# A TensorE-bound kernel in three-term fp32r: tiles padded to lines of 256 bytes, and the last gate and up columns as one block

## The chip, the cores and the metric

The kernel runs on one core of one Trainium2 chip. The metric is the time of one execution on the device, in microseconds; where several runs are compared, their median.

The five engines run side by side and meet at semaphores. In the profile, PE is TensorE's matmuls and PEld its loads of the stationary operand; DVE is VectorE, ACT ScalarE, POOL GpSimd, and SP the engine that here only issues DMAs. PSUM, into which matmuls write, has eight banks for each partition; one bank holds 512 fp32 columns. SBUF is addressed by a partition and by a byte within it. "Residue" below is a start address within the partition modulo 256.

## What is computed

One batch of 256 tokens of width 1024 runs through three layers; each is a feed-forward part, a mixer and another feed-forward part, all in fp32. The feed-forward part has six uses, and its hidden width is 2816, that is five blocks of 512 columns and one of 256:

```python
D_FF = 2816
def swiglu(x, w_gate, w_up, w_down):
    return (jax.nn.silu(x @ w_gate) * (x @ w_up)) @ w_down
...
    for l in range(DEPTH):
        f1 = swiglu(rms_norm(x, ffn1_pre_g[l]), ffn1_w_gate[l], ffn1_w_up[l], ffn1_w_down[l])
        x = x + FFN_RESIDUAL_WEIGHT * rms_norm(f1, ffn1_post_g[l])
        m = token_mixer(rms_norm(x, mix_pre_g[l]), w_in[l], fox_forget_b[l],
...
        x = x + rms_norm(m, mix_post_g[l])
        f2 = swiglu(rms_norm(x, ffn2_pre_g[l]), ffn2_w_gate[l], ffn2_w_up[l], ffn2_w_down[l])
```

The mixer of the first layer holds two kinds of softmax attention; that of the two others has three branches (stick breaking, block attention, sparse attention), gates of 3 x 1024 columns and an output projection. For the change the mixers matter as more matrix products of the same form.

## The kernel before

**Tiling.** The tokens are two blocks `t` of 128. A weight matrix comes in units of 128 partitions (rows) times at most some 1024 columns of fp32, that is 512 KB: `wtiles` (L203) takes `step = 1100 // n` row tiles of `n` columns into one unit, so two row tiles for n = 512, four for n = 256 and four for n = 264. The down and output projections load one row tile of 1024 columns as a unit.

**Three terms.** A product in fp32 accuracy is made of three matmuls in fp32r. `load` (L186) brings a unit by one DMA from SP's queue (L190) into a buffer `raw`, ACT rounds it to `hi` (L198), and DVE subtracts to get `lo` (L200). The activations are split the same way into `xh` and `xl` (or `ah` and `al` in the down projection). `mm3` (L211) issues hi with xh (L213), lo with xh (L214) and hi with xl (L215). The weight tile is the moving operand, which streams through the array, 512 columns wide as a rule; the activation tile of 128 columns is the stationary one, loaded ahead of each matmul (PEld). A unit of 1024 columns is thus 12 matmuls of 512 columns: two halves, two token blocks, three terms. TensorE runs in the order written here, apart from small pieces of other work that the scheduler of the language puts between.

**Buffers and addresses.** `raw`, `hi` and `lo` have four buffers each (RAW, HILO), used in turn. A buffer is as large as the largest tile of its tag: the 4 x 264 columns of the forget gates' projection, 4224 bytes, which is 16.5 x 256. Small tiles that lie ahead (`mhalf` and `eps` of 4 bytes, `gT` of 32) shift all that follows. In the built program `xh` and `xl` begin at residue 32 (96 in one place of the mixers); `hi` and `lo` begin, buffer by buffer in turn, at 32, 160, 32, 160; `ah` and `al` begin at 224. The last four units of a down projection have buffers of their own (MORE), at 224. The columns of a tile are whole multiples of 256 bytes away from its start in nearly all these matmuls, so an operand has its tile's residue.

Units of 12 matmuls in a row with one weight tile, counted in the built program: in the gate and up columns of the feed-forward parts 108 at residue 32 and 108 at 160; in the down projections 42 at 32 and 42 at 160; in the gates and projections of the mixers 37 at 32 and 37 at 160. The rest are halves of six matmuls, where one token block goes ahead of the other: about 80 of them lie at 160.

**The feed-forward part** (`ffn`, L338). For each block of 512 columns gate (`g`) and up (`u`) are two `dense` products of 48 matmuls, into two PSUM tiles `mm` (three banks in turn) and two `at` (two banks). Then ACT makes `sg = silu(g)` (L362), DVE `a = u * sg` (L364). `flush` (L346) transposes the `a` of the block before on TensorE, four pieces for each token block into `tp` (two banks) and `po` (one bank), from which ACT casts `ah` (L252) and DVE makes `al` (L253); it runs between gate and up of the next block. The last block has 256 columns: 48 matmuls of 256 columns for gate, the transposes of block five, 48 of 256 for up, and then the transposes of the last block itself. `out_proj` (L671) follows with 22 units of 12 matmuls into two `mm` and two `at`.

Of the kernel before, what the change touches and what calls it, by code (L numbers as in the profile page):

```python
# [8 lines left out]
F32 = mybir.dt.float32  # L9
F32R = mybir.dt.float32r  # L10
BF = mybir.dt.bfloat16
# [5 lines left out]
P = 128  # L17
# [11 lines left out]
MORE = 4  # L29

# ---------------------------------------------------------------- constants that depend on shapes only
# [85 lines left out]
class K:  # L117
    def __init__(self, ctx, tc, d):
# [15 lines left out]
        self.x = []  # L134
        for t in range(2):
            xt = self.cpool.tile([P, D], F32, name=f"x{t}")
            nc.sync.dma_start(out=xt, in_=d["x"][0, t * P:(t + 1) * P, :])
            self.x.append(xt)
# [4 lines left out]
        self.mhalf = self.cpool.tile([P, 1], F32, name="mhalf")  # L143
        nc.vector.memset(self.mhalf, -0.5)
        self.eps = self.cpool.tile([P, 1], F32, name="eps")
        nc.vector.memset(self.eps, EPS)

    def consts(self):
        cf = self.cpool.tile([P, F32_W], F32, name="cf")
# [14 lines left out]
    def tile(self, pool, shape, tag, dt=F32, bufs=None):  # L164
        kw = {} if bufs is None else {"bufs": bufs}
        return pool.tile(shape, dt, tag=tag, name=self.nm(tag), **kw)
# [13 lines left out]
    def sm(self, w, tag="sm"):  # L180
        if tag == "rs":
            return self.tile(self.small, [P, w], tag)
        return self.tile(self.small, [P, 32 if w > 8 else 8], "sm32" if w > 8 else "sm", bufs=2 if w > 8 else 24)[:, :w]

    # ------------------------------------------------------------ weights
    def load(self, w, r0, nk, c0, n, pool=None):  # L186
        """rows r0.. (nk tiles of 128), cols c0..c0+n, split exactly into hi + lo."""
        nc = self.nc
        raw = self.tile(self.wpool, [P, nk, n], "raw", bufs=RAW)
        nc.sync.dma_start(out=raw, in_=w[r0:r0 + nk * P, c0:c0 + n].rearrange("(k p) n -> p k n", p=P))  # L190
# [12 lines left out]
    def wtiles(self, w, r0, nk, c0, n):  # L203
        """the K tiles of load(), one by one, in units of at most 1024 columns."""
        step = max(1, 1100 // n)
# [11 lines left out]
    def dense(self, ps, xs, w, c0, n, skew=False):  # L217
        """ps[t] = x[t] @ w[:, c0:c0 + n]; with skew token block 0 goes ahead of token block 1."""
# [14 lines left out]
    # ------------------------------------------------------------ norms  # L233
    def rsqrt(self, out, ss, scale, eps):
        """out = (ss * scale + eps) ** -0.5"""
# [9 lines left out]
    def split_T(self, src, hi, lo, k0=0, bank=None):  # L245
        """transpose 512 columns of src (f32, token-major) into hi/lo[:, k0:k0+4]."""
# [8 lines left out]
    def prenorm(self, t, g):  # L255
        """transposed x*g (hi, lo) and the per-token 1/rms."""
# [15 lines left out]
    def first_norms(self, gd):  # L272
        """prenorm() of both token blocks, the gain put on after the transposes."""
# [5 lines left out]
        gT = self.cpool.tile([P, 8], F32, name="gT")  # L279
# [26 lines left out]
    def prenorms(self, gd):  # L306
        """transposed inputs of a part; the part before has left them, but for the very first."""
# [5 lines left out]
    def finish(self, t, ps, weight, post):  # L313
        """x[t] += weight * (rmsnorm(f) * post, or f)."""
# [22 lines left out]
    # ------------------------------------------------------------ feed forward  # L337
    def ffn(self, gd, wg, gc0, wu, uc0, wd, postd, nxt):  # L338
# [3 lines left out]
        with tc.tile_pool(name=self.nm("ffn"), bufs=1) as fp:  # L342
# [8 lines left out]
            for c0 in range(0, FF, 512):  # L351
                n = min(512, FF - c0)
                ps = {}
                for name, w, base in (("g", wg, gc0), ("u", wu, uc0)):
                    for t in range(2):
                        ps[name, t] = self.mm((P, n)) if name == "g" else self.at((P, n))
                    self.dense([ps[name, t] for t in range(2)], xs, w, base + c0, n, c0 == 0 and name == "g")
                    if name == "g":
                        flush()
# [18 lines left out]
    # ------------------------------------------------------------ pieces of the mixers  # L378
    def small_gain(self, pool, g, reps, tag):
        """[P, reps, n] copy of a vector of n on every partition."""  # L380
# [16 lines left out]
    def rope(self, x, cos, sin, half):  # L397
        """x: [P, G, >=2*half] in place; cos, sin: [P, 2*half], sin with its sign."""
# [10 lines left out]
    def head_rs(self, sq, n):  # L409
        """1 / rms of the last axis, from the squares [P, G, n]: exp and ln, then a step of Newton's."""  # L410
# [14 lines left out]
    def head_norm(self, out, x, s, g):  # L425
        """out = rms norm of s * x over the last axis of [P, G, n], gains g; s: one scalar per token."""
# [766 lines left out]
```

## Time and profile before

| | |
|---|---|
| median of three runs | 1811.75 us (1810.66 to 1812.93) |
| the profiled execution: its time is its span, first to last instruction | 1813.0 us |
| PE busy | 1790.0 us, 99% |
| PEld busy | 1471.7 us, 81% |
| DVE busy | 1079.1 us, 60% |
| ACT busy | 895.2 us, 49% |
| DMA | 305 MB, mean 168 GB/s |

The profiled execution lies at the upper end of the three timed ones, 1.25 us above their median. Of a matmul the start is measured, and its end is modelled; matmuls overlap in the pipeline, so a duration of 0.39 us is not the time that one costs. What a matmul costs is the distance from its start to the start of the next, which the timeline gives to 0.01 us.

### The profile page before, as it was taken

The numbers are of one execution on the slowest core, as the hardware profiler recorded it, in microseconds if no ns is written. First come the engines' busy times: TensorE is split into PE (matmuls) and PEld (weight loads), VectorE is DVE, ScalarE is ACT, GpSimd is POOL, SyncE is SP. The second block draws the span as 40 slices with busy tenths as digits, with TensorE's granted clock in tenths as the row PEclk, the third lists the DMA queues.
The fourth block names the chain that finished last, engine by engine and source line by source line (L and its number), as shares of the span: only waits on it lengthen the run. The fifth ranks groups of instructions, "written<-read, shape, count | busy, mean of one in ns | idle before, by whom it ended". The sixth has DMA issues, their size and how long they took to land.

```text
span 1813.0 us, 23411 instructions
## 1 busy us (share of the span) xinstructions
PE 1790.0 (99%) x8875; PEld 1471.7 (81%) x8883; DVE 1079.1 (60%) x1705; ACT 895.2 (49%) x1358; POOL 25.9 (1%) x42
## 2 busy tenths in 40 slices
PE   8999999999999999999999999999999999999999
PEld 6888787788878888787888888888887878888887
DVE  5555565555555555797567555555556975575553
ACT  5444455444445444475555444444444755554442
POOL 0000100000000000000000000000000000000000
PEclk9999999999999999999999999999999999999999
DMA  8665644266556655544255665666555442546653
GB/s 271 185 185 184 189 134 147 83 205 180 183 186 187 185 177 183 155 141 127 71 174 176 207 186 177 201 180 182 178 185 156 140 129 70 174 163 207 181 181 128
DMA packets 154594, 305.11 MB, mean 168 GB/s; under 512 B 13641, under 2 KB 44945, under 8 KB 154481
## 3 DMA queue, kind: packets, MB, share of 16 engines
q1 hardware_dynamic: 154464, 303.61, 54.6%
q8 instruction: 70, 1.15, 0.3%
q14 instruction: 44, 0.35, 0.1%
q10 hardware_dynamic: 16, 0.00, 0.0%
HBM read 302.53 MB, written 1.05 MB: 167 GB/s over the span
## 4 chain that ended last, share of the span: by engine, by line
PE 93%; DVE 3%; DMA 2%; ACT 1%; issue 1%; SPq 0%; POOL 0%; POOLq 0%; ACTq 0%
PE mm_ffn L215 10%; PE mm_ffn L214 10%; PE mm_ffn L213 10%; PE at_ffn L215 10%; PE at_ffn L214 10%; PE at_ffn L213 10%; PE mm_gate L214 3%; PE mm_gate L215 2%; PE mm_gate L213 2%; PE at_nsa L475 1%; PE mm_m L214 1%; PE mm_m L213 1%; PE mm_m L215 1%; PE po_nsa L505 1%; PE tp_ffn L251 1%; PE po_ffn L251 1%
## 5 line engine op out<-in xcount | busy, mean ns | idle before, releaser
L200 DVE TENSOR_TENSOR lo_ffn<-raw_ffn,hi_ffn 128x1024 fp32r<-128x1024 f32 x396 | 482.8, 1224 | 477.9 <-ACT hi_ffn L198 477.2
L198 ACT CAST hi_ffn<-raw_ffn 128x1024 fp32r<-128x1024 f32 x396 | 413.3, 1048 | 523.5 <-PE at_ffn L215 337.8
L213 PE MATMUL mm_ffn<-hi_ffn,xh_ffn 128*128 128x512 f32 (+1 forms) x288 | 109.3, 379 | 2.0 <-ACT xh_ffn L292 1.1
L213 PE MATMUL at_ffn<-hi_ffn,xh_ffn 128*128 128x512 f32 (+1 forms) x288 | 109.0, 379 | 0.0
L215 PE MATMUL mm_ffn<-hi_ffn,xl_ffn 128*128 128x512 f32 (+1 forms) x288 | 108.8, 378 | 0.0
L214 PE MATMUL mm_ffn<-lo_ffn,xh_ffn 128*128 128x512 f32 (+1 forms) x288 | 108.8, 378 | 0.0
L215 PE MATMUL at_ffn<-hi_ffn,xl_ffn 128*128 128x512 f32 (+1 forms) x288 | 107.8, 374 | 0.0
L214 PE MATMUL at_ffn<-lo_ffn,xh_ffn 128*128 128x512 f32 (+1 forms) x288 | 107.7, 374 | 0.0
L215 PE MATMUL mm_ffn<-hi_ffn,al_ffn 128*128 128x512 f32 x264 | 104.5, 396 | 0.0
L215 PE MATMUL at_ffn<-hi_ffn,al_ffn 128*128 128x512 f32 x264 | 104.1, 394 | 0.0
L214 PE MATMUL at_ffn<-lo_ffn,ah_ffn 128*128 128x512 f32 x264 | 104.0, 394 | 0.0
L213 PE MATMUL mm_ffn<-hi_ffn,ah_ffn 128*128 128x512 f32 x264 | 103.8, 393 | 0.0
L214 PE MATMUL mm_ffn<-lo_ffn,ah_ffn 128*128 128x512 f32 x264 | 103.5, 392 | 0.0
L213 PE MATMUL at_ffn<-hi_ffn,ah_ffn 128*128 128x512 f32 x264 | 103.5, 392 | 0.0
L200 DVE TENSOR_TENSOR lo_gate<-raw_gate,hi_gate 128x1024 fp32r<-128x1024 f32 x48 | 58.5, 1218 | 36.2 <-ACT hi_gate L198 36.2
L214 PE MATMUL mm_gate<-lo_gate,xh_ffn 128*128 128x512 f32 x192 | 77.4, 403 | 0.6 <-DVE lo_gate L200 0.6
L213 PE MATMUL mm_gate<-hi_gate,xh_ffn 128*128 128x512 f32 x192 | 77.1, 402 | 0.0
L215 PE MATMUL mm_gate<-hi_gate,xl_ffn 128*128 128x512 f32 x192 | 76.8, 402 | 0.0
L213 PE MATMUL at_ffn<-hi_ffn,xh_wo 128*128 128x512 f32 (+1 forms) x192 | 72.7, 379 | 0.0
L214 PE MATMUL mm_ffn<-lo_ffn,xh_wo 128*128 128x512 f32 (+1 forms) x192 | 72.0, 375 | 0.0
L215 PE MATMUL mm_ffn<-hi_ffn,xl_wo 128*128 128x512 f32 (+1 forms) x192 | 71.9, 375 | 0.0
L215 PE MATMUL at_ffn<-hi_ffn,xl_wo 128*128 128x512 f32 (+1 forms) x192 | 71.8, 374 | 0.0
(562 smaller groups left out, 3965.6 us busy)
## 6 DMA issues: line engine op xcount, KB each, us to landing
raw_ffn<-in_ffn_w_gu_dram SPq DMA_DIRECT2D x176, 512.0 KB, 3.7
raw_ffn<-in_ffn_w_down_dram SPq DMA_DIRECT2D x132, 512.0 KB, 3.4
raw_gate<-in_w_gate_dram SPq DMA_DIRECT2D x48, 512.0 KB, 3.7
raw_ffn<-in_ffn_w_gate_dram SPq DMA_DIRECT2D x44, 512.0 KB, 3.9
raw_ffn<-in_ffn_w_up_dram SPq DMA_DIRECT2D x44, 512.0 KB, 3.8
raw_m<-in_w_in_dram SPq DMA_DIRECT2D x22, 512.0 KB, 4.1
raw_wo<-in_w_out_dram SPq DMA_DIRECT2D x16, 512.0 KB, 3.5
raw_sb<-in_w_in_dram SPq DMA_DIRECT2D x12, 512.0 KB, 4.5
```

What stands on the lines that cost most here:

```text
L198: nc.scalar.copy(hi, raw)
L200: nc.vector.tensor_sub(lo, raw, hi.bitcast(F32))
L213: nc.tensor.matmul(out, xh, wh, start=first, stop=False)
L214: nc.tensor.matmul(out, xh, wl, start=False, stop=False)
L215: nc.tensor.matmul(out, xl, wh, start=False, stop=last)
L251: nc.tensor.transpose(p[:, i], src[:, i * P:(i + 1) * P], self.ident)
L475: nc.tensor.matmul(sc[:, i, c], q, k[:, c], start=False, stop=i == len(heads) - 1 and b in (t, None))
L505: self.nc.tensor.matmul(out, PT[:, i * (t + 1) + b], v(b), start=b == 0, stop=b == t)
```

## The change

Every tile that the helper `tile` makes (outside PSUM and the pool of small tiles) is rounded up to a multiple of 256 bytes for each partition, and the view of the wanted shape is cut out of it. The few small tiles made without the helper are gathered: `mhalf`, `eps` and `gT` become columns of one tile `misc` of 256 bytes, the four scaled 1/rms vectors of the second mixer become `rsv`, and an unused tile `skip` of 128 bytes fills the line that is open at the start. `wtiles` takes at most 1024 columns, so the 264 columns of the forget gates come as units of 3, 3 and 2 row tiles and not of 4 and 4, and the buffers `raw`, `hi` and `lo` have 4096 bytes. In the built program all 512-column operands, moving and stationary, begin at residue 0.

The last block of the feed-forward part is one product: 256 gate and 256 up columns stand side by side in `raw`, loaded by two DMAs of 256 KB, and 48 matmuls of 512 columns make both into one `mm` bank for each token block. The matmuls of the program fall from 8460 to 8172.

```diff
+LINE = 256
...
+        self.cpool.tile([P, 32], F32, name="skip")
...
-        self.mhalf = self.cpool.tile([P, 1], F32, name="mhalf")
+        self.misc = self.cpool.tile([P, 64], F32, name="misc")
+        self.mhalf, self.eps = self.misc[:, 0:1], self.misc[:, 1:2]
         nc.vector.memset(self.mhalf, -0.5)
-        self.eps = self.cpool.tile([P, 1], F32, name="eps")
...
     def tile(self, pool, shape, tag, dt=F32, bufs=None):
         kw = {} if bufs is None else {"bufs": bufs}
-        return pool.tile(shape, dt, tag=tag, name=self.nm(tag), **kw)
+        free = int(np.prod(shape[1:]))
+        unit = LINE // (2 if dt == BF else 4)
+        full = -(-free // unit) * unit
+        if pool is self.psum or pool is self.small or full == free:
+            return pool.tile(shape, dt, tag=tag, name=self.nm(tag), **kw)
+        t = pool.tile([shape[0], full], dt, tag=tag, name=self.nm(tag), **kw)[:, :free]
...
+        return t
...
         raw = self.tile(self.wpool, [P, nk, n], "raw", bufs=RAW)
-        nc.sync.dma_start(out=raw, in_=w[r0:r0 + nk * P, c0:c0 + n].rearrange("(k p) n -> p k n", p=P))
+        parts, m = ([(w, c0)], n) if not isinstance(w, list) else (w, n // len(w))
+        for i, (v, c) in enumerate(parts):
+            nc.sync.dma_start(out=raw[:, :, m * i:m * i + m],
+                              in_=v[r0:r0 + nk * P, c:c + m].rearrange("(k p) n -> p k n", p=P))
...
-        step = max(1, 1100 // n)
+        step = max(1, 1024 // n)
...
+                else:
+                    both = [self.mm((P, 2, n)) for t in range(2)]
+                    ps = {(name, t): both[t][:, i] for t in range(2) for i, name in enumerate("gu")}
+                    self.dense([v.rearrange("p a n -> p (a n)") for v in both], xs,
+                               [(wg, gc0 + c0), (wu, uc0 + c0)], 0, 2 * n)
+                    flush()
```

TensorE at the end of the first feed-forward part, before: the last matmuls of `up` (tile `at`, 256 columns), the transposes of the last block (`a_ffn_1146` and `a_ffn_1152`, one for each token block), and the first of the down projection (`mm_ffn_1168` and later).

```order
590 L214 MATMUL at_ffn_1083<-lo_ffn_1117,xh_ffn_115 128x256
591 L215 MATMUL at_ffn_1083<-hi_ffn_1116,xl_ffn_116 128x256
592 L251 MATMUL tp_ffn_1156<-ident,a_ffn_1146 128x128 x2
593 L213 MATMUL mm_ffn_1168<-hi_ffn_1174,ah_0_ffn_302 128x512
594 L214 MATMUL mm_ffn_1168<-lo_ffn_1175,ah_0_ffn_302 128x512
595 L251 MATMUL po_ffn_1161<-ident,a_ffn_1152 128x128 x2
```

The same place after the change; `mm_ffn_1006` now holds gate and up of token block 1, and `a_ffn_995` and `a_ffn_1001` are those of block five.

```order
541 L229 MATMUL mm_ffn_1006<-hi_ffn_1067,xl_ffn_115 128x512
542 L265 MATMUL tp_ffn_1083<-ident,a_ffn_995 128x128 x4
543 L265 MATMUL po_ffn_1090<-ident,a_ffn_1001 128x128 x4
544 L227 MATMUL mm_ffn_1121<-hi_ffn_1127,ah_0_ffn_301 128x512
545 L265 MATMUL tp_ffn_1109<-ident,a_ffn_1099 128x128 x2
546 L228 MATMUL mm_ffn_1121<-lo_ffn_1128,ah_0_ffn_301 128x512
...
557 L227 MATMUL mm_ffn_1121<-hi_ffn_1145,ah_0_ffn_301 128x512
558 L265 MATMUL po_ffn_1114<-ident,a_ffn_1105 128x128 x2
```

Both flushes now stand behind the last block: the transposes of block five directly behind it, those of the last block one matmul and thirteen matmuls into the down projection. Two uses of the one `po` bank, which stood 48 matmuls apart, now stand 13 apart.

DVE at that place, before: the lower parts `al` of block five (`al_0_ffn_999`, `al_1_ffn_1005`) are made ahead of the products `a` of the last block.

```order
79 L253 TENSOR_TENSOR al_0_ffn_999<-tp_ffn_1068,ah_0_ffn_998 128x512
80 L253 TENSOR_TENSOR al_1_ffn_1005<-po_ffn_1075,ah_1_ffn_1004 128x512
81 L200 TENSOR_TENSOR lo_ffn_1211<-raw_ffn_1208,hi_ffn_1210 128x1024
82 L364 SCALAR_TENSOR_TENSOR a_ffn_1146<-at_ffn_1082,rs_ffn_138,sg_ffn_1144 128x256
83 L364 SCALAR_TENSOR_TENSOR a_ffn_1152<-at_ffn_1083,rs_ffn_144,sg_ffn_1150 128x256
```

After, on DVE:

```order
79 L214 TENSOR_TENSOR lo_ffn_1164<-raw_ffn_1161,hi_ffn_1163 128x1024
80 L385 SCALAR_TENSOR_TENSOR a_ffn_1099<-mm_ffn_1005,rs_ffn_137,sg_ffn_1097 128x256
81 L385 SCALAR_TENSOR_TENSOR a_ffn_1105<-mm_ffn_1006,rs_ffn_143,sg_ffn_1103 128x256
82 L214 TENSOR_TENSOR lo_ffn_1182<-raw_ffn_1179,hi_ffn_1181 128x1024
83 L267 TENSOR_TENSOR al_0_ffn_998<-tp_ffn_1083,ah_0_ffn_997 128x512
84 L267 TENSOR_TENSOR al_1_ffn_1004<-po_ffn_1090,ah_1_ffn_1003 128x512
```

The products of the last block now come first, and a weight unit's `lo` stands ahead of the subtraction that frees `po` (`al_1_ffn_1004`).

## Rows read from the trace of the kernel before

**Rows 1.** The page: busy time; clock in 40 slices; the chain that ended last.

```profile
PE 1790.0 (99%) x8875; PEld 1471.7 (81%) x8883; DVE 1079.1 (60%) x1705; ACT 895.2 (49%) x1358; POOL 25.9 (1%) x42
...
PEclk9999999999999999999999999999999999999999
...
PE 93%; DVE 3%; DMA 2%; ACT 1%; issue 1%; SPq 0%; POOL 0%; POOLq 0%; ACTq 0%
```

**Rows 2.** PE's waits: who waited for what, us in total, times, longest.

```profile
PE tp_pn L735 <- DMA pe_pn<-in_nsa_cmp_pe_dram: 6.6, 2, 3.5
PE mm_m L214 <- DVE lo_m L200: 2.7, 1, 2.7
```

**Rows 3.** Timeline, PE: units' first matmuls, one up block; start us, us, what.

```profile
98.80 0.39 PE L213 MATMUL at_ffn<-hi_ffn,xh_ffn 128*128 128x512 f32 x1
...
101.53 0.40 PE L213 MATMUL at_ffn<-hi_ffn,xh_ffn 128*128 128x512 f32 x1
...
104.33 0.39 PE L213 MATMUL mm_ffn<-hi_ffn,xh_ffn 128*128 128x512 f32 x1
```

**Rows 4.** The same of a later feed-forward part, whose blocks begin in another buffer.

```profile
1025.07 0.40 PE L213 MATMUL at_ffn<-hi_ffn,xh_wo 128*128 128x512 f32 x1
...
1027.86 0.39 PE L213 MATMUL at_ffn<-hi_ffn,xh_wo 128*128 128x512 f32 x1
...
1030.59 0.40 PE L213 MATMUL mm_ffn<-hi_ffn,xh_wo 128*128 128x512 f32 x1
```

**Rows 5.** The same in a down projection, one weight row tile a unit.

```profile
154.14 0.39 PE L213 MATMUL mm_ffn<-hi_ffn,ah_ffn 128*128 128x512 f32 x1
...
156.93 0.39 PE L213 MATMUL mm_ffn<-hi_ffn,ah_ffn 128*128 128x512 f32 x1
...
159.68 0.39 PE L213 MATMUL mm_ffn<-hi_ffn,ah_ffn 128*128 128x512 f32 x1
```

**Rows 6.** Timeline, PE: the last block, gate from 127.33, up from 133.83.

```profile
127.33 0.28 PE L213 MATMUL mm_ffn<-hi_ffn,xh_ffn 128*128 128x256 f32 x1
...
133.04 0.60 PE L251 MATMUL tp_ffn<-ident,a_ffn 128*128 128x128 f32 x4
133.47 0.60 PE L251 MATMUL po_ffn<-ident,a_ffn 128*128 128x128 f32 x4
133.83 0.36 PE L213 MATMUL at_ffn<-hi_ffn,xh_ffn 128*128 128x256 f32 x1
...
139.52 0.28 PE L215 MATMUL at_ffn<-hi_ffn,xl_ffn 128*128 128x256 f32 x1
139.79 0.44 PE L251 MATMUL tp_ffn<-ident,a_ffn 128*128 128x128 f32 x2
139.98 0.48 PE L213 MATMUL mm_ffn<-hi_ffn,ah_ffn 128*128 128x512 f32 x1
140.30 0.40 PE L214 MATMUL mm_ffn<-lo_ffn,ah_ffn 128*128 128x512 f32 x1
```

**Rows 7.** Timeline, ACT, behind the gate columns of the last block.

```profile
133.24 0.47 ACT L362 ACTIVATE sg_ffn<-mm_ffn,rs_ffn 128x256 f32<-128x256 f32 x1 [0.95 <-PE mm_ffn L215]
133.61 1.04 ACT L198 CAST hi_ffn<-raw_ffn 128x1024 fp32r<-128x1024 f32 x1
134.55 0.59 ACT L252 CAST ah_ffn<-tp_ffn 128x512 fp32r<-128x512 f32 x1
```

**Rows 8.** Timeline, DVE, the same place.

```profile
134.68 1.23 DVE L200 TENSOR_TENSOR lo_ffn<-raw_ffn,hi_ffn 128x1024 fp32r<-128x1024 f32 x1 [1.99 <-ACT hi_ffn L198]
135.82 0.68 DVE L253 TENSOR_TENSOR al_ffn<-tp_ffn,ah_ffn 128x512 fp32r<-128x512 f32 x1
136.42 0.68 DVE L253 TENSOR_TENSOR al_ffn<-po_ffn,ah_ffn 128x512 fp32r<-128x512 f32 x1
```

**Rows 9.** Timeline, SP: issues of the last block's gate loads; DMA issues, us to landing.

```profile
109.59 3.16 SPq L190 DMA_DIRECT2D raw_ffn<-in_ffn_w_gate_dram  x2
...
raw_ffn<-in_ffn_w_gate_dram SPq DMA_DIRECT2D x44, 512.0 KB, 3.9
```

More of the change, by code (lines that the diff above doesn't have):

```diff
@@ L142, in __init__ @@
                                 fill=1.0, base=0, channel_multiplier=1)
-        self.mhalf = self.cpool.tile([P, 1], F32, name="mhalf")
+        self.misc = self.cpool.tile([P, 64], F32, name="misc")
+        self.mhalf, self.eps = self.misc[:, 0:1], self.misc[:, 1:2]
         nc.vector.memset(self.mhalf, -0.5)
-        self.eps = self.cpool.tile([P, 1], F32, name="eps")
         nc.vector.memset(self.eps, EPS)
     def consts(self):
-        cf = self.cpool.tile([P, F32_W], F32, name="cf")
+        cf = self.tile(self.cpool, [P, F32_W], "cf")
         cb = self.cpool.tile([P, BF_W], BF, name="cb")
@@ L165, in tile @@
         kw = {} if bufs is None else {"bufs": bufs}
-        return pool.tile(shape, dt, tag=tag, name=self.nm(tag), **kw)
+        free = int(np.prod(shape[1:]))
[4 more added lines that the diff above has]
+        t = pool.tile([shape[0], full], dt, tag=tag, name=self.nm(tag), **kw)[:, :free]
+        if len(shape) > 2:
+            names = "abcd"[:len(shape) - 1]
+            t = t.rearrange(f"p ({' '.join(names)}) -> p {' '.join(names)}", **dict(zip(names, shape[1:])))
+        return t
     def mm(self, shape=(P, 512)):
@@ L181, in sm @@
         if tag == "rs":
-            return self.tile(self.small, [P, w], tag)
+            return self.tile(self.small, [P, w], tag, bufs=8)
         return self.tile(self.small, [P, 32 if w > 8 else 8], "sm32" if w > 8 else "sm", bufs=2 if w > 8 else 24)[:, :w]
@@ L278, in first_norms @@
         nc.tensor.transpose(gp, gt, self.ident[:8, :8])
-        gT = self.cpool.tile([P, 8], F32, name="gT")
+        gT = self.misc[:, 8:16]
         nc.vector.tensor_copy(gT, gp)
@@ L352, in ffn @@
                 n = min(512, FF - c0)
[L353 to L359, printed above, removed]
+                if n == 512:
+                    ps = {}
+                    for name, w, base in (("g", wg, gc0), ("u", wu, uc0)):
+                        for t in range(2):
+                            ps[name, t] = (self.mm if name == "g" else self.at)((P, n))
+                        self.dense([ps[name, t] for t in range(2)], xs, w, base + c0, n, c0 == 0 and name == "g")
+                        if name == "g":
+                            flush()
[4 more added lines that the diff above has]
+                               [(wg, gc0 + c0), (wu, uc0 + c0)], 0, 2 * n)
+                    flush()
                 for t in range(2):
@@ L737, in mixer2 @@
             rs8, rsh = [], []
+            rsv = L([P, 4], "rsv")
             for t in range(2):
-                a = L([P, 1], f"rs8_{t}")
+                a = rsv[:, 2 * t:2 * t + 1]
                 nc.vector.tensor_scalar(out=a, in0=xs[t][2], scalar1=0.125, scalar2=None, op0=OP.mult)
-                b = L([P, 1], f"rsh_{t}")
+                b = rsv[:, 2 * t + 1:2 * t + 2]
                 nc.vector.tensor_scalar(out=b, in0=xs[t][2], scalar1=0.5, scalar2=None, op0=OP.mult)
```

## The prediction

> **What bounds the kernel now.** I read the page first, then PE's waits, then the timeline at three places. The page says that TensorE is busy for 1790.0 of 1813.0 us, at the full clock (2.4 GHz) in all 40 slices, and that the chain which ended last is PE for 93% [rows 1]. What PE waits for is short and named: 6.6 us for two small DMAs in the mixers, 2.7 us once for a weight's lower part [rows 2]. So there is hardly an idle stretch to win. What remains is how fast matmul follows matmul, and for that the duration of a row (0.39 us) says nothing; the distance between starts does.
>
> That distance isn't the same everywhere. A unit is 12 matmuls on one weight tile. In an up block the unit from 98.80 takes 2.73 us and the one from 101.53 takes 2.80 [rows 3]: the same shapes, the same engine, the same clock. The buffers of the weights alternate between residue 32 and residue 160, and xh and xl lie at 32, so the first is a unit whose streamed and loaded operands have one residue, and the second one whose operands are 128 bytes apart. It could also be the place in the block, since every block has four units and the buffers are four. A later feed-forward part decides this: there the third unit of the block lies at 160, and it takes 2.79 us, the fourth lies at 32 and takes 2.73 [rows 4]. The longer unit follows the buffer. In the down projection ah and al lie at 224; the unit at 160 takes 2.79 us and the one at 32 takes 2.75 [rows 5]: neither has the residue of the stationary operand, and both take longer than 2.73. I conclude that a matmul costs 227.5 ns where stream and weight load have one residue, about 229 at 64 bytes of distance, and 232.5 at 128 or 192.
>
> **Part one: one residue for all.** The change puts every 512-column operand at residue 0. No row shows a matmul with both operands at 0; what the rows show is the distance, and I price the new state with the units of distance 0, that is 2.73 us.
>
> - Gate and up columns: 108 full units at 160 (distance 128), 0.06 us each by [rows 3, 4]: 6.5 us.
> - Gates and projections of the mixers: 37 such units, 2.2 us.
> - Down projections: 42 units at 160 from 2.79 to 2.73, 2.5 us; 42 units at 32 from 2.75 to 2.73, 0.8 us [rows 5].
> - About 80 half units, where six matmuls of one token block follow each other and the rows of full units do not apply: between nothing and 80 times 0.03 us, 2.4 us. I take 0.5.
>
> Together 12.5 us, all of it on PE, which is the path. The bounds: half of it, if the distance modulo 256 is only part of what makes a unit longer; and 2 us more from the half units. DVE and ACT need 1.23 and 1.04 us for a unit [rows 7, 8], so at 2.73 us a unit they stay behind PE with more than a microsecond to spare; nothing of the gain is taken back there. Matmuls of the attention and the transposes get new residues too. They are fp32, in small groups, and no row sets two residues of one of them side by side; I take 0, with 1.5 us either way.
>
> A rule of the skill speaks against this whole part. The Trainium skill, "TensorE: Matmul & The Clock Gate", section "Step-by-step: what each phase is for", says that TensorE has two independent SBUF read ports and that loading the next tile's weights "doesn't steal SBUF read bandwidth from the running matmul". By that rule no start address could matter, and part one would be worth nothing. The rows at 2.73 and 2.80 us differ where only the addresses do, so the trace disagrees, by 2%.
>
> **Part two: the last block as one product.** Before, gate takes 127.33 to 133.04, 5.71 us, and up 133.83 to 139.79, 5.96 us; together 11.67 for 96 matmuls of 256 columns [rows 6]. The 5.96 hold two things of their own. The first matmul behind fp32 transposes costs about 0.1 us more (139.98 to 140.30 is 0.32 and not 0.23), which after the change falls on the down projection instead. And the transposes at 139.79 start 0.27 us behind the last matmul, where 0.12 is the rule: a wait of 0.15 us for the product `a`. After the change 48 matmuls of 512 columns are four units, 4 x 2.735 = 10.94 us. The gain is 11.67 - 0.10 - 10.94 = 0.63 us with the wait in it, 3.8 us for six feed-forward parts. The count of other switches between transposes and products stays the same.
>
> The order brings a new meeting point. Both flushes now follow the block, and `po` has one bank: the transposes of the last block need it from `al` of block five. With T as the start of the first transposes, PE comes there at T + 0.43 + 0.36 + 0.32 + 0.19 + 0.32 + 11 x 0.228 = T + 4.13 us (all steps in [rows 6]). The other side: silu of token block 1 starts 0.20 us behind the next matmul's start (133.04 to 133.24), the weight cast 0.37 later, the first `ah` 0.94 after that, the second some 0.5 later, T + 2.0 [rows 6, 7]. DVE starts the weight's `lo` as the cast ends, at T + 1.64, the first `al` 1.14 later, the second 0.60 after that, and ends it 0.68 later: T + 4.06 [rows 8]. That is a tie. I charge 0.1 us for each part, 0.6 in all; it could be nothing, or 0.6 each, 3.6 in all. The transposes of token block 0 wait for nothing: their sums end six matmuls ahead of T, 1.37 us, and they are due at T + 1.1, so silu, a `lo` and `a` have 2.5 us.
>
> The loads are split in two DMAs of 256 KB. Gate's loads for the last block are issued at 109.59, 17.7 us ahead of their first use at 127.33, and land after 3.9 us [rows 6, 9]; eight issues in place of four cost nothing under that cover. Without it each would cost PE up to one landing. The forget gates' third load is one more cast of the smallest kind on engines with slack; what it does to the order in the first mixer I put at 0, with 1 us either way.
>
> **The sum.** 1813.0 - 12.5 - 3.8 + 0.6 = 1797.3 us in terms of the profiled execution. That one lies 1.25 us above the median of the runs, so 1796.0 in terms of the median.
>
> **The rivals.**
>
> (a) Residues don't matter, and something else that goes with a buffer makes every second unit longer (its place beyond the line of 256 bytes, say). Only part two is left: 1813.0 - 3.2 = 1809.8, in the median 1808.5. The rule of the Trainium skill quoted above would give this time. For it: I have only two sets of residues for most units. Against it: the down projection, where both kinds of units change when the stationary operand is at 224.
>
> (b) Residue 0 is itself the costly place: if a start on a line of 256 bytes makes stream and weight load meet at each line's first bytes, the units of 2.73 us pay what those of 2.79 us do. The 145 full units at distance 0 would go from 2.73 to 2.79, 8.7 us more, the 42 of the down projections from 2.75, 1.7 us, nothing is gained on the units that take 2.79 us now, and part two is left with 4 x 2.79 in its block, 1.9 us after the charge at `po`: 1813.0 + 8.7 + 1.7 - 1.9 = 1821.5, in the median 1820, slower than before. It decides once about two thirds of the 374 full units take 2.79 us: today half of them are, and part two pays for some 50 more. Against it: the rows price distances alike for 32 and 224, which says that the distance counts and not the place.
>
> (c) Half of part one: all weight tiles now have one phase at 4096 bytes too, which the old pitch of 4224 did not give. 6 us less gain: 1802.
>
> (d) The meeting at `po` comes late by 0.6 us and more in each part, and with it the clock or the weights' lead suffer: 3 to 8 us, 1799 to 1804.
>
> (e) The change doesn't reach all operands. The built program's addresses exclude that for the 512-column matmuls.
>
> **How the numbers follow.** Forecast, 1790.5 to 1800: 0.74. Cases (c) and (d) up to 1803: 0.10, beyond it 0.04. Case (a): 0.05. Case (b): 0.04. Better than 1790.5, if the half units and the attention gain as well: 0.03. The range reaches over the forecast and the nearer part of (c) and (d), 1790.5 to 1803, which leaves out 0.16. What a measurement of this kernel can tell from no change is about 0.2%, 3.6 us, so "faster" ends at 1808.1: the forecast, (c), (d), the better case and a part of (a) give 0.92; the rest of (a) is "same", 0.04; (b) is "slower", 0.04.
>
> **What would show it.** In the profile after, the starts of successive units should be 2.73 to 2.74 us apart in every block, gate and up as in the down projection, with no alternation; that is part one. If every unit takes 2.79, (b) is right, and if the alternation stays, (a). The last block should take 10.9 us and its two flushes follow; the distance ahead of the last `po` transposes tells the tie: 0.23 us if nothing waits, more if `al` of block five is late. PE's waits should hold the same two lines at the top. The prediction is wrong above all if 0 is not like 32 and 224.

## The result and the profile after

The changed kernel takes 1791.03 us (median of four runs, 1789.05 to 1793.97) against 1812.34 us for the kernel before (1810.66 to 1814.83); the ratio is 0.9886, with an interval of 0.9872 to 0.9899. The forecast was 1796.0 us in a range of 1790.5 to 1803.0, so the time lies inside it, half a microsecond from its lower end. The direction and the mechanism were right. The gain was larger than the sum: 21.3 us by the medians, 24.1 us between the two profiled spans, where the sum had 15.7. That the time is still inside the range is owed to the room below the forecast, 5.5 us, of which 5.0 were needed. Each ratio below is to the kernel before, timed beside the kernel in question (its medians: 1812.34 to 1813.89 us).

One correction to how the profiled execution of before was read ahead of the prediction: its span of 1813.0 us is not all of its time. A time is some 1.8 us more than its span (1790.69 us and 1788.9 in the changed kernel), so that execution is the one of 1814.83 us, the longest of the four. The working below compares spans, 24.1 us, of which some 2.5 us are that one long execution.

The page of the changed kernel: span, busy time, TensorE's clock in 40 slices, the chain that ended last. It answers [rows 1].

```profile
span 1788.9 us, 22896 instructions
...
PE 1765.3 (99%) x8595; PEld 1453.9 (81%) x8595; DVE 1079.4 (60%) x1706; ACT 897.2 (50%) x1359; POOL 25.8 (1%) x42
...
PEclk9999999999999999999999999999999999999999
...
PE 93%; DVE 3%; DMA 2%; ACT 1%; issue 1%; SPq 0%; POOL 0%; POOLq 0%; ACTq 0%
```

PE lost 24.7 us of busy time; VectorE and ScalarE did what they did before. TensorE's granted clock was the same in both profiled executions, 0.993 in the mean; that is not the full clock throughout, as the prediction read it, since a 9 in the row of slices stands for 90% and more. So the gain lies in PE's own stream: in fewer matmuls in the last block, and in how fast matmul follows matmul. PE's two longest waits are those of [rows 2]:

```profile
PE tp_pn L756 <- DMA pe_pn<-in_nsa_cmp_pe_dram: 6.6, 2, 3.5
PE mm_m L228 <- DVE lo_m L214: 2.7, 1, 2.7
```

The timeline of PE, first matmuls of successive units (start in us, modelled duration, what): the end of the up block of [rows 3] and the block behind it, a later feed-forward part as in [rows 4], the down projection of [rows 5].

```profile
99.18 0.39 PE L227 MATMUL at_ffn<-hi_ffn,xh_ffn 128*128 128x512 f32 x1
...
101.90 0.39 PE L227 MATMUL mm_ffn<-hi_ffn,xh_ffn 128*128 128x512 f32 x1
...
104.62 0.39 PE L227 MATMUL mm_ffn<-hi_ffn,xh_ffn 128*128 128x512 f32 x1
...
1011.41 0.39 PE L227 MATMUL at_ffn<-hi_ffn,xh_wo 128*128 128x512 f32 x1
...
1014.13 0.39 PE L227 MATMUL at_ffn<-hi_ffn,xh_wo 128*128 128x512 f32 x1
...
150.68 0.39 PE L227 MATMUL mm_ffn<-hi_ffn,ah_ffn 128*128 128x512 f32 x1
...
153.40 0.39 PE L227 MATMUL mm_ffn<-hi_ffn,ah_ffn 128*128 128x512 f32 x1
```

Every step is 2.72 us. Of the 318 full units that no transpose interrupts, 287 take 2.72 us to within 5 ns. Before, they alternated between 2.735 and 2.79 (2.75 and 2.79 in the down projections). The level is not only even, as forecast; it is lower than the lowest one that I had priced.

The last block, which answers [rows 6]: its first matmul, its last, the transposes of both flushes, and the last use of `po`.

```profile
124.58 0.39 PE L227 MATMUL mm_ffn<-hi_ffn,xh_ffn 128*128 128x512 f32 x1
...
135.47 0.60 PE L265 MATMUL tp_ffn<-ident,a_ffn 128*128 128x128 f32 x4
135.90 0.60 PE L265 MATMUL po_ffn<-ident,a_ffn 128*128 128x128 f32 x4
136.26 0.48 PE L227 MATMUL mm_ffn<-hi_ffn,ah_ffn 128*128 128x512 f32 x1
136.71 0.44 PE L265 MATMUL tp_ffn<-ident,a_ffn 128*128 128x128 f32 x2
...
139.53 0.39 PE L227 MATMUL mm_ffn<-hi_ffn,ah_ffn 128*128 128x512 f32 x1
139.76 0.38 PE L265 MATMUL po_ffn<-ident,a_ffn 128*128 128x128 f32 x2
```

And the subtraction on DVE that frees `po` there, which answers the end of [rows 8]:

```profile
138.85 0.68 DVE L267 TENSOR_TENSOR al_ffn<-po_ffn,ah_ffn 128x512 fp32r<-128x512 f32 x1
```

The block takes 10.89 us (124.58 to 135.47). With T = 135.47, `al` ends at T + 4.06, to the hundredth what the prediction worked out, and PE reaches the last transposes at T + 4.29, 0.23 us behind the matmul ahead of them: these wait for nothing. The tie at `po` went PE's way by 0.23 us.

### The profile page after: what moved, and what is told of

The parts are those of the page before. It is cut to its first block, busy times and chain, and to the rows that moved or that the text cites. A ratio compares the mean times of both kernels' runs of the same rounds, so it can differ in the third digit from the quotient of the medians.

```text
span 1788.9 us, 22896 instructions
## 1 busy us (share of the span) xinstructions
PE 1765.3 (99%) x8595; PEld 1453.9 (81%) x8595; DVE 1079.4 (60%) x1706; ACT 897.2 (50%) x1359; POOL 25.8 (1%) x42
## 4 chain that ended last, share of the span: by engine, by line
PE 93%; DVE 3%; DMA 2%; ACT 1%; issue 1%; SPq 0%; POOL 0%; POOLq 0%; ACTq 0%
PE mm_ffn L227 10%; PE mm_ffn L229 10%; PE mm_ffn L228 10%; PE at_ffn L229 9%; PE at_ffn L227 9%; PE at_ffn L228 9%; PE mm_gate L228 3%; PE mm_gate L229 2%; PE mm_gate L227 2%; PE at_nsa L496 1%; PE mm_m L228 1%; PE mm_m L227 1%; PE mm_m L229 1%; PE po_nsa L526 1%; PE tp_ffn L265 1%; PE po_ffn L265 1%
## 5 line engine op out<-in xcount | busy, mean ns | idle before, releaser
L227 PE MATMUL mm_ffn<-hi_ffn,xh_ffn 128*128 128x512 f32 x288 | 113.1, 393 | 2.5 <-ACT xh_ffn L306 1.3
L228 PE MATMUL mm_ffn<-lo_ffn,xh_ffn 128*128 128x512 f32 x288 | 112.8, 392 | 0.0
L229 PE MATMUL mm_ffn<-hi_ffn,xl_ffn 128*128 128x512 f32 x288 | 112.7, 391 | 0.0
L227 PE MATMUL at_ffn<-hi_ffn,xh_ffn 128*128 128x512 f32 x240 | 94.5, 394 | 0.0
L229 PE MATMUL at_ffn<-hi_ffn,xl_ffn 128*128 128x512 f32 x240 | 93.5, 390 | 0.0
L228 PE MATMUL at_ffn<-lo_ffn,xh_ffn 128*128 128x512 f32 x240 | 93.4, 389 | 0.0
L228 PE MATMUL mm_ffn<-lo_ffn,xh_wo 128*128 128x512 f32 x192 | 74.9, 390 | 0.0
L229 PE MATMUL mm_ffn<-hi_ffn,xl_wo 128*128 128x512 f32 x192 | 74.7, 389 | 0.0
L227 PE MATMUL mm_ffn<-hi_ffn,xh_wo 128*128 128x512 f32 x192 | 74.7, 389 | 0.0
L212 ACT CAST hi_gate<-raw_gate 128x1024 fp32r<-128x1024 f32 x48 | 50.4, 1051 | 40.1 <-PE mm_gate L229 38.4
```

The costliest lines, as they stand in the source:

```text
L212: nc.scalar.copy(hi, raw)
L227: nc.tensor.matmul(out, xh, wh, start=first, stop=False)
L228: nc.tensor.matmul(out, xh, wl, start=False, stop=False)
L229: nc.tensor.matmul(out, xl, wh, start=False, stop=last)
```

## The experiments

Theory A is that of the prediction: the time between matmuls depends on the distance, modulo 256 bytes, between the start of the streamed operand (`hi`, `lo`) and that of the loaded one (`xh`, `xl`, `ah`, `al`). Its rivals: B, the place counts, and a start on a line of 256 bytes is better or worse as such; C, the pitch of 4096 bytes or the padding of other tiles does it; D, the merge brought the gain; E, what counts is how `hi` and `lo` lie against the tiles that ACT and DVE read or that DMA writes.

### The two parts, each alone

Padding without the merged block:

```diff
-                if n == 512:
+                if n:
```

> The changed kernel without the merged block: the last 256 gate and 256 up columns are two products again, the padding stays. What the two traces give for the merge: from the start of the last block to the third unit of the down projection 18.52 us before and 17.94 after, of which 0.10 us is the first two down units, so 0.48 us for a part and 2.9 us for six. Expected 1791.0 + 2.9 = 1793.9 us, all full units at 2.72 us. If the forecast's own term for the merge was right (3.2 us without a charge at po 3.8): 1794.2 to 1794.8. If the merge and not the padding had brought most of the gain, this kernel would be near 1809.

Measured: 1794.41 us, ratio to the kernel before 0.9897 (0.9878 to 0.9916); units of 2.72 us. The merge without the padding, in the kernel before:

```diff
-        nc.sync.dma_start(out=raw, in_=w[r0:r0 + nk * P, c0:c0 + n].rearrange("(k p) n -> p k n", p=P))
+        parts, m = ([(w, c0)], n) if not isinstance(w, list) else (w, n // len(w))
+        for i, (v, c) in enumerate(parts):
+            nc.sync.dma_start(out=raw[:, :, m * i:m * i + m],
+                              in_=v[r0:r0 + nk * P, c:c + m].rearrange("(k p) n -> p k n", p=P))
...
+                else:
+                    both = [self.mm((P, 2, n)) for t in range(2)]
+                    ps = {(name, t): both[t][:, i] for t in range(2) for i, name in enumerate("gu")}
+                    self.dense([v.rearrange("p a n -> p (a n)") for v in both], xs,
+                               [(wg, gc0 + c0), (wu, uc0 + c0)], 0, 2 * n)
+                    flush()
```

> The kernel before with the merged block alone; tiles, pitches and residues stay, so units go on alternating between 2.735 and 2.79 us. The merge is worth 2.9 us less what the dearer units take back in its block (two of four at 2.79, two at 2.735, 0.17 us a part, 1.0 us): 1.9 to 2.9 us, 1809.4 to 1810.4 us. If parts one and two only work together, 1812.

Measured: 1808.92 us, ratio 0.9976 (0.9965 to 0.9987), which is 4.4 us (2.4 to 6.3), a little more than the 1.9 to 2.9 expected. Its units alternate as they did in the kernel before (PE, first matmuls of the last unit of an up block and of the two behind it; 2.79, then 2.74 us):

```profile
98.72 0.40 PE L216 MATMUL at_ffn<-hi_ffn,xh_ffn 128*128 128x512 f32 x1
...
101.51 0.39 PE L216 MATMUL mm_ffn<-hi_ffn,xh_ffn 128*128 128x512 f32 x1
...
104.25 0.40 PE L216 MATMUL mm_ffn<-hi_ffn,xh_ffn 128*128 128x512 f32 x1
```

D falls: the padding alone brings 18.7 us (1.03%) and the merge alone 4.4. The merge's own worth lies between 2.9 us, from the two traces, and 4.4 (3.4 by the medians of pad_only and the changed kernel); the interval is too wide for more.

### Distance or place

All operands at residue 32 and none at 0:

```diff
-        self.cpool.tile([P, 32], F32, name="skip")
+        self.cpool.tile([P, 40], F32, name="skip")
```

> The changed kernel with the first unused tile 32 bytes longer, so that every operand lies at residue 32 and none at 0. Theory A, only the distance between the streamed and the loaded operand counts: units of 2.72 us as in the changed kernel, 1791 us. Theory B, the start of a 256-byte line counts: at least the 2.735 us of the units at 32 before, 374 x 0.015 = 5.6 us and half as much for the half units, 1797 to 1800 us; or 2.79 for all, 1820 us.

Measured: 1791.38 us, ratio 0.9886 (0.9864 to 0.9907), the same as the changed kernel. Timeline of PE, units' first matmuls:

```profile
99.86 0.39 PE L227 MATMUL at_ffn<-hi_ffn,xh_ffn 128*128 128x512 f32 x1
...
102.58 0.39 PE L227 MATMUL mm_ffn<-hi_ffn,xh_ffn 128*128 128x512 f32 x1
...
105.30 0.39 PE L227 MATMUL mm_ffn<-hi_ffn,xh_ffn 128*128 128x512 f32 x1
```

2.72 us, although nothing begins on a line. B falls. Padding to lines matters only because it makes all residues alike.

Weights moved by 128 bytes, pitch still 4096:

```diff
+    def gap(self, pool, size, name):
+        if size and name not in self.gaps:
+            self.gaps.add(name)
+            pool.tile([P, size // 4], F32, name=name, bufs=1)
...
+            self.gap(self.wpool, 128, "gap1")
             hi = self.tile(self.wpool, [P, nk, n], "hi", F32R, bufs=HILO)
             lo = self.tile(self.wpool, [P, nk, n], "lo", F32R, bufs=HILO)
+            self.gap(self.wpool, 128, "gap3")
```

> The changed kernel with a gap of 128 bytes ahead of the hi buffers and one behind the lo buffers: the streamed weights lie at residue 128, xh, xl, ah, al at 0, the pitch of the buffers stays 4096. About 5900 of the 6300 wide matmuls are 128 bytes apart; the eight last loads of the large output projections lie in another pool and stay at 0. Theory A: a unit at distance 128 cost 0.072 us more than 2.72 before and the unit behind it 0.015, so 6.0 to 7.2 ns a matmul, 35 to 43 us: 1826 to 1834 us, all units alike near 2.79 to 2.81, and the half units of those eight loads at 1.36. Theory C, it was the pitch of 4096 instead of 4224 or the padding of other tiles: no change, 1791 us.

Measured: 1819.97 us, ratio 1.0036 (1.0024 to 1.0048): not only is the gain gone, the kernel is 6.5 us longer than before, since now all units and not every second one are 128 bytes apart. Two units of an up block:

```profile
99.79 0.39 PE L235 MATMUL at_ffn<-hi_ffn,xh_ffn 128*128 128x512 f32 x1
...
102.58 0.40 PE L235 MATMUL at_ffn<-hi_ffn,xh_ffn 128*128 128x512 f32 x1
...
105.36 0.40 PE L235 MATMUL mm_ffn<-hi_ffn,xh_ffn 128*128 128x512 f32 x1
```

C falls. The size was over-estimated: 28.9 us between the spans over the 5904 matmuls that lie 128 bytes apart in the built program are 4.9 ns each, not 6.0 to 7.2. The last loads of each output projection, which stayed at 0 (four of them, and not eight as expected), ended in half units of 1.36 us in the same kernel.

The loaded operands moved instead, the weights left at 0:

```diff
+            self.gap(self.xpool, 128, "gap")
             hi = self.tile(self.xpool, [P, 8, P], f"xh{t}", F32R)
             lo = self.tile(self.xpool, [P, 8, P], f"xl{t}", F32R)
+            if t:
+                self.gap(self.xpool, 128, "gapend")
```

> The changed kernel with a gap of 128 bytes ahead of xh and xl, so that these loaded operands lie at residue 128, while the weights (raw, hi, lo), ah, al and the operands of the output projections stay at 0. About 4500 wide matmuls are 128 bytes apart, all those of the down projections are not. Theory A, distance between stream and weight load: 5.2 ns a matmul as w128 showed (29.6 us for 5700), 23.5 us, 1814 to 1815 us; units of the gate, up and mixer products near 2.79 us, those of the down projections 2.72. Theory E, what counted in w128 was the place of hi and lo against the raw tiles that ACT and DVE read: no change, 1791 us, all units 2.72.

Measured: 1812.71 us, ratio 0.9997 (0.9988 to 1.0007). Its timeline has both kinds of units, first two starts of an up block, then two of the down projection, whose `ah` and `al` were not moved:

```profile
99.62 0.39 PE L233 MATMUL at_ffn<-hi_ffn,xh_ffn 128*128 128x512 f32 x1
...
102.42 0.39 PE L233 MATMUL at_ffn<-hi_ffn,xh_ffn 128*128 128x512 f32 x1
...
154.74 0.39 PE L233 MATMUL mm_ffn<-hi_ffn,ah_ffn 128*128 128x512 f32 x1
...
157.46 0.39 PE L233 MATMUL mm_ffn<-hi_ffn,ah_ffn 128*128 128x512 f32 x1
```

2.80 us and 2.72 us. E falls: in the built program no tile but `xh` and `xl` has changed its residue, and the whole gain is gone. This is the experiment that carries theory A: two kernels with the same instructions, 22.6 us apart in their spans (21.7 by the medians) where 23.5 were forecast, by 128 bytes in the place of `xh` and `xl`. Over the 4512 matmuls concerned that is 5.0 ns each, as in w128.

### How the price depends on the distance

The gap ahead of `hi` changed to 32, 64, 192 and 224 bytes, and the one behind `lo` to the rest of 256; for 64, against w128:

```diff
-            self.gap(self.wpool, 128, "gap1")
+            self.gap(self.wpool, 64, "gap1")
...
-            self.gap(self.wpool, 128, "gap3")
+            self.gap(self.wpool, 192, "gap3")
```

> As w128 with 64 bytes in place of 128. The kernel before had this distance in its down projections (32 against 224): 2.751 us a unit, of which up to 0.015 us may come from the neighbour at 160. By theory A a unit is 0.016 to 0.031 us above 2.72, over 475 units' worth of matmuls 8 to 15 us: 1799 to 1806 us. If any distance costs the same: 1820 us.

> As w128 with 192 bytes. The kernel before had 192 in its down projections (160 against 224): 2.789 us, like 128. Theory A with a distance that is counted in one direction (stream minus load, modulo 256): 2.79 us a unit, 1818 to 1820 us. If only the nearer way round counted (192 is 64 backwards), it would be as w64.

> As w128 with 32 bytes. w64 cost 0.027 us a unit, w192 0.080. If the cost grows with the distance from the first byte on: 0.013 us a unit, 2.733 us, 475 units: 1797 us. If it comes in steps of 64 bytes: 2.720 us and 1791, or 2.747 us and 1802.

> As w128 with 224 bytes, which is 32 bytes short of the next common residue. If the cost grows with the directed distance (stream minus load, modulo 256: 0.027 at 64, 0.071 at 128, 0.080 at 192): 2.80 to 2.81 us a unit, 1823 to 1829 us. If 32 bytes backwards count as little as 32 forwards: as w32, 1791 to 1802 us.

| distance | time, us | ratio to before | a full unit, us |
|---|---|---|---|
| 0 (changed kernel) | 1791.03 | 0.9886 (0.9872 to 0.9899) | 2.720 |
| 32 | 1823.68 | 1.0049 (1.0032 to 1.0066) | 2.800 |
| 64 | 1802.09 | 0.9943 (0.9927 to 0.9959) | 2.747 |
| 128 | 1819.97 | 1.0036 (1.0024 to 1.0048) | 2.780 to 2.800, median 2.791 |
| 192 | 1823.20 | 1.0063 (1.0046 to 1.0080) | 2.800 |
| 224 | 1823.38 | 1.0050 (1.0035 to 1.0065) | 2.800 |

Timeline of PE, units in an up block at distance 64, then at 32:

```profile
98.31 0.39 PE L235 MATMUL at_ffn<-hi_ffn,xh_ffn 128*128 128x512 f32 x1
...
101.06 0.39 PE L235 MATMUL at_ffn<-hi_ffn,xh_ffn 128*128 128x512 f32 x1
```

```profile
100.60 0.39 PE L235 MATMUL at_ffn<-hi_ffn,xh_ffn 128*128 128x512 f32 x1
...
103.40 0.39 PE L235 MATMUL at_ffn<-hi_ffn,xh_ffn 128*128 128x512 f32 x1
```

The expectations for 64 and 224 held, that for 192 was exceeded by 3 us; the one for 32 failed in all its forms (1791 to 1802 expected). A distance of 32 bytes is as dear as any. The price does not grow with the distance; 64 bytes are cheap and the other distances that were run are dear. The expectation of w224 by growth (1823 to 1829) held in its number, and w32 shows that growth is not the reason.

### Only one of three matmuls off

A gap between `hi` and `lo` (the middle matmul's stream is off), and gaps between `xh` and `xl` (the third one's load is off):

```diff
             hi = self.tile(self.wpool, [P, nk, n], "hi", F32R, bufs=HILO)
+            self.gap(self.wpool, 128, "gap2")
             lo = self.tile(self.wpool, [P, nk, n], "lo", F32R, bufs=HILO)
+            self.gap(self.wpool, 128, "gap3")
```

```diff
             hi = self.tile(self.xpool, [P, 8, P], f"xh{t}", F32R)
+            self.gap(self.xpool, 128, f"gapl{t}")
             lo = self.tile(self.xpool, [P, 8, P], f"xl{t}", F32R)
+            self.gap(self.xpool, 128, f"gape{t}")
```

> The changed kernel with the gap between the hi and the lo buffers: only the lower parts of the weights lie at residue 128, so the middle matmul of each three streams at distance 128 and the two others at 0. If each matmul pays for itself, a third of w128's cost: 29 / 3 = 9.7 us, 1801 us, and the middle matmul or the one behind it is the longer one. If each return from 128 to 0 costs the 15 ns that the units behind the 160 ones showed: up to 1900 x 15 ns = 28 us more, up to 1829 us. If the first address of a whole unit mattered and not that of each matmul: 1791 us.

> The changed kernel with 128 bytes between xh and xl: of each three matmuls of the gate, up and mixer products only the third loads an operand at residue 128; all streams and all other loads stay at 0. In lo128 it was the stream that changed its residue at each step, and a whole unit then took 2.747, 2.773 or 2.80 us. Theory A, distance between stream and load, in whichever operand: the same levels here, units of 2.747 to 2.80 us in the gate, up and mixer products (376 units' worth of matmuls), 2.72 in the down projections: 1791 + 10 to 30, most likely 1801 to 1812 us. Theory F, lo128 was dear because successive streams lay differently: 1791 us and 2.72 everywhere.

Measured: 1817.94 us for lo128, ratio 1.0034 (1.0022 to 1.0046), and 1807.14 us for xl128, ratio 0.9968 (0.9956 to 0.9979). In lo128 units of the same shape and the same residues hold three different levels, one after the other. From its timeline of PE: a unit of the first up block, of the next block, of the down projection.

```profile
98.42 0.40 PE L235 MATMUL at_ffn<-hi_ffn,xh_ffn 128*128 128x512 f32 x1
...
101.22 0.40 PE L235 MATMUL at_ffn<-hi_ffn,xh_ffn 128*128 128x512 f32 x1
...
121.64 0.40 PE L235 MATMUL at_ffn<-hi_ffn,xh_ffn 128*128 128x512 f32 x1
...
124.41 0.40 PE L235 MATMUL at_ffn<-hi_ffn,xh_ffn 128*128 128x512 f32 x1
...
156.33 0.39 PE L235 MATMUL mm_ffn<-hi_ffn,ah_ffn 128*128 128x512 f32 x1
...
159.08 0.39 PE L235 MATMUL mm_ffn<-hi_ffn,ah_ffn 128*128 128x512 f32 x1
```

2.80, 2.77 and 2.75 us; the level changes at the transposes of a flush, which interrupt the stream, and holds from one to the next. In xl128 a unit takes 2.773 us, and 2.72 in the down projection. By the times, one operand of three that lies apart costs 16.1 us (xl128, against 21.7 for both `xh` and `xl`) and 26.9 us (lo128, against 28.9 for both `hi` and `lo`): three quarters and more, not a third. The matmuls do not pay one by one. That the streams differ among themselves is not needed for it (xl128 has all of them at 0), so theory F of that expectation falls as the only reason; whether it adds to lo128, the dearer of the two, is not shown. Which of the three matmuls carries the stall cannot be read off: in lo128 the median distances from one start to the next are 235, 234 and 230 ns, in xl128 227, 232 and 234, so matmuls whose own operands have one residue take longer than 227 too.

### A wait that was left

The trace after leaves PE's wait for `pe_pn` at the top. Its load stands ninth among small loads on the same queue; moved to the first place:

```diff
+            pe = T([32, P], "pe")
+            nc.sync.dma_start(out=pe, in_=G("nsa_cmp_pe").rearrange("v (m r) d -> (v m) (r d)", r=2))
             gA = T([P, 5, 64], "gA")
...
-            pe = T([32, P], "pe")
-            nc.sync.dma_start(out=pe, in_=G("nsa_cmp_pe").rearrange("v (m r) d -> (v m) (r d)", r=2))
```

> The changed kernel with one small load moved: the 16 KB of pe, for which PE waits 3.2 us in each of the two parts that use it, is issued ahead of eight other small loads on the same queue (721.5 us, the ninth, in the profile after; the first goes at 718.1) and not behind them. It should land up to 3.4 us earlier: 5 to 6.5 us less in all, 1784.5 to 1786 us. If its landing is set by what the other loads keep the engines busy with and not by its place in the queue, nothing: 1791 us. The residues stay at 0, units at 2.72 us.

Measured: 1782.23 us, ratio to the kernel before 0.9824 (0.9807 to 0.9842), so it beats the changed kernel too (0.9886, 0.9872 to 0.9899). PE's waits are now headed by the other line, and `pe_pn` is not among them:

```profile
PE mm_m L228 <- DVE lo_m L214: 3.2, 1, 3.2
PE tp_ffn L292 <- DMA gt<-in_ffn_pre_g_dram: 2.3, 1, 2.3
```

The median lies below the 1784.5 to 1786 expected: the medians differ by 8.8 us, the wait was 6.6. The two places themselves give the rest. From the last matmul of the third down projection to the first of the fourth the changed kernel takes 378.9 us and this one 374.4, and from the fifth to the sixth 379.2 and 374.4, so 9.3 us in all. What goes beyond the wait, 2.7 us, lies behind it, in TensorE's clock. PE in the changed kernel, two matmuls of 296 columns ahead of the wait, the transpose that waited, and two of 296 columns behind it:

```profile
724.00 0.30 PE L228 MATMUL mm_ix<-lo_ix,xh_ffn 128*128 128x296 f32 x1
724.14 0.30 PE L229 MATMUL mm_ix<-hi_ix,xl_ffn 128*128 128x296 f32 x1
727.61 0.28 PE L756 MATMUL tp_pn<-ident,pe_pn 32*128 32x32 f32 x1 [3.17 <-DMA pe_pn<-in_nsa_cmp_pe_dram]
...
728.48 0.45 PE L229 MATMUL mm_ix<-hi_ix,xl_ffn 128*128 128x296 f32 x1
728.72 0.45 PE L227 MATMUL mm_ix<-hi_ix,xh_ffn 128*128 128x296 f32 x1
```

They follow each other in 0.14 us ahead of the wait and in 0.24 to 0.25 behind it. The granted clock is 1.00 from 721 to 725 and 0.50, the lower level of 1.2 GHz, from 727.5 to 730.5; behind the second wait it is 0.50 again (1355.5 to 1358.5). In pe_first, where PE doesn't wait there, it is 1.00 at both places (722 to 731 and 1340 to 1352).

The spans differ by 4.8 us only, because the profiled execution of pe_first, the longest of its four (1785.95 us), lost the rest where the edit changes nothing: from the first down projection to the second, which holds the first mixer, it takes 273.1 us and the changed kernel 269.6.

## Why the prediction was right, and where its sum was short

**The mechanism held.** That the longer units come from operands 128 bytes apart was read from [rows 3 to 5] alone, and x128 shows it directly. Theory A was confirmed at places that the kernel before could not show: the place of all operands together doesn't matter (0 in the changed kernel, 32 in all32), and moving either operand alone undoes the gain (w128, x128). The Trainium skill, "TensorE: Matmul & The Clock Gate", section "Step-by-step: what each phase is for", says that loading the next weights takes nothing from the running matmul's reads of SBUF. Here the trace disagrees: in x128 the place of the loaded operand alone costs 22.6 us. That the two reads collide is the nearest explanation; the runs show the dependence on the distance, not the collision itself.

**The sum, term by term**, from the two profiled spans:

| term | forecast, us | measured, us |
|---|---|---|
| 145 units at distance 0, gate, up, mixers | 0 | 145 x 0.015 = 2.2 |
| 145 units at distance 128 there | 8.7 | 145 x 0.072 = 10.4 |
| 84 units of the down projections | 3.3 | 42 x 0.069 + 42 x 0.031 = 4.2 |
| half units | 0.5 | 192 x 0.0177 = 3.4 |
| merged block, with `po` | 3.8 - 0.6 = 3.2 | 6 x 0.48 = 2.9 |
| sum | 15.7 | 23.1 of 24.1 |

That the sum comes so close to 24.1 is in part chance. Single spans scatter by some us: from the first down projection to the second all32 takes 267.1 us, the changed kernel 269.6 and pe_first 273.1, with the same units. By the medians the gain is 21.3 us; where the other 1.8 us go is not shown.

The step that failed is the sentence "I price the new state with the units of distance 0, that is 2.73 us". The 2.73 of [rows 3] was not the price of distance 0; it held an after-effect of the unit ahead of it, at distance 128. The kernel before shows it, if one looks inside that unit. Its triples of matmuls, on the timeline of PE between the rows of [rows 3]:

```profile
99.49 0.39 PE L213 MATMUL at_ffn<-hi_ffn,xh_ffn 128*128 128x512 f32 x1
...
100.17 0.39 PE L213 MATMUL at_ffn<-hi_ffn,xh_ffn 128*128 128x512 f32 x1
...
100.85 0.39 PE L213 MATMUL at_ffn<-hi_ffn,xh_ffn 128*128 128x512 f32 x1
```

From 98.80, the start of the unit, the first three matmuls take 0.69 us, and the three triples behind them 0.68 each, to 101.53. Four times 0.68 is 2.72. The trace of before also had this price in the open, and the prediction passed it over. In a down projection the buffers at 224 meet `ah` and `al` at the same residue, for 48 matmuls each time. The last two half units of the first down projection, and the matmul behind them:

```profile
199.91 0.39 PE L213 MATMUL at_ffn<-hi_ffn,ah_ffn 128*128 128x512 f32 x1
...
201.27 0.39 PE L213 MATMUL at_ffn<-hi_ffn,ah_ffn 128*128 128x512 f32 x1
...
202.63 0.39 PE L213 MATMUL mm_m<-hi_m,xh_ffn 128*128 128x512 f32 x1
```

Six matmuls take 1.36 us there, half of 2.72. With that price the full units give 16.8 us (2.2 + 10.4 + 4.2) where the forecast had 12.0.

The second mis-sized term is that of the half units. "I take 0.5" was a choice near the lower bound because the rows of full units "do not apply"; its upper bound of 2.4 us counted only the some 80 at residue 160. Of the 227 half units 192 run without an interruption or a wait in both kernels: the 67 of them at 160 fall by 0.026 us each, 1.7 us, which the bound allows, and the 125 others, for which the sum had nothing, by 0.013, another 1.7 us.

**The merge** came out nearly at its size, in part by luck: the block takes 10.89 us where 10.94 was worked out, and 0.6 us was charged to the wrong tile. The charge at `po` (0.1 us a part) did not fall due. What fell due was a wait that the prediction had excluded ("The transposes of token block 0 wait for nothing"). DVE's two products `a`, and PE's weight load for those transposes:

```profile
136.17 0.92 DVE L385 SCALAR_TENSOR_TENSOR a_ffn<-mm_ffn,rs_ffn,sg_ffn 128x256 f32<-128x256 f32 x2 [0.92 <-ACT sg_ffn L383]
...
136.71 0.20 PEld L265 LDWEIGHTS tp_ffn<-ident,a_ffn 128*128 128x128 f32 x2 [0.29 <-DVE a_ffn L385]
```

DVE makes both products only behind the second silu; the first is there at T + 1.18, and the transposes were due at T + 1.1. Why it didn't begin behind the first silu is not shown. The step from the first down matmul to the transposes behind it was put at 0.32 us and takes 0.45 (136.26 to 136.71), in each of the six parts: 0.8 us in all. The same delay gave `al` 0.23 us to spare at `po` and not the 0.07 of the working (4.13 less 4.06). The loads stayed covered, as said.

**The rivals.** (a), only the merge counts: refuted by pad_only and x128. (b), residue 0 is itself costly: refuted by the result and by all32, whose time at 32 is the same. (c), a phase at 4096 bytes takes back half: not seen, 287 of the 318 full units take 2.72. (d), `po` late: not seen. (e): excluded by the addresses, and the units bear it out.

**What the prediction said that was not right beyond this kernel:** "about 229 at 64 bytes of distance, and 232.5 at 128 or 192" was read from alternating units. Steadily it is 228.9 at 64 (2.747 / 12), 232.6 at 128 and 233.3 at 192. Nor is a small distance cheap, as the 229 at 64 may suggest: at 32 bytes a matmul costs 233.3 ns.

## What to carry to other kernels

Where TensorE is busy all the time, look at the starts of successive matmuls of one shape, not at their durations: two levels for the same shape are a question to be asked of the addresses, and a level must be read behind a few matmuls of its own kind, because the neighbour's residue reaches into it (for three matmuls in the unit from 98.80). Give all streamed and all loaded operands of wide products the same start modulo 256 bytes, be it 0 or 32; one tile of odd length in a pool shifts all those behind it, and one operand of three out of place already cost three quarters of the price and more. Padding can do harm as easily: with the weights 32 bytes off (w32) this kernel is 0.5% longer than before.

## What the runs showed of the hardware that I had not expected

- Any of the distances run but 0 costs; 32 bytes (2.800 us a unit) as much as 192 and 224, and 64 the least (2.747).
- The units settle on few levels: 2.720, 2.747, 2.773 and 2.800 us, steps of 27 ns in twelve matmuls, 6.7 ns in three. In lo128 units with the same residues hold each of the upper three for a whole stretch, and the level changes where transposes come between. Distance 128 in all three matmuls (w128, x128) is an exception, with 2.780 to 2.800 from unit to unit. What sets the level at such an interruption stays open.
- Twice 128 is no distance: 284 matmuls of the changed kernel, in the mixers, whose operands are an odd multiple of 256 bytes apart, follow each other in 226.9 ns on average, like the others that nothing interrupts (227.2).
- A wait of PE can cost more than itself: the two for `pe_pn` (3.17 and 3.46 us) took 9.3 us with the stretches at 1.2 GHz behind them, which were gone when the waits were.
